# Attention outputs taken in alternating halves, and a distance penalty moved from a matrix product to VectorE

## The chip, the cores and the metric

The kernel runs on one core of one Trainium2 chip. The time is the device time of one execution in microseconds (us); of the kernel before three runs are known, with a median of 1116.42 us (1116.35 to 1116.87). The trace of one further, profiled execution gives what every engine did: PE is TensorE's matrix product, PEld its weight load, DVE is VectorE, ACT ScalarE, POOL GpSimd, SP the engine that issues most DMAs.

## The reference, cut to what matters

Two layers; each has a half-step SwiGLU feed-forward, a token mixer with two attention branches, and a second feed-forward. There are 256 tokens of width 1024, all in float32. Only the mixer is touched:

```python
def gqa_attention(q, k, v):            # branch A: 8 query heads, 2 key/value heads of 64
    sc = einsum(q, k) * 64 ** -0.5
    p = softmax(sc)
    return einsum(p, v)

def diff_attention(q, k, v, lam, slopes):   # branch B: 4 heads, two softmax maps each
    dist = abs(qpos[:, None] - kpos[None, :])
    bias = -slopes[:, None, None] * dist[None]
    sc = einsum(q, k) * 64 ** -0.5
    p = softmax(sc + bias[None, None])
    w = p[:, 0] - lam * p[:, 1]
    return einsum(w, v)
```

`slopes` is 2^(-2), 2^(-4), 2^(-6), 2^(-8) for the four heads.

## The kernel before

Weights arrive from HBM in tiles of 128x2048 float32. Each half tile (128x1024) is split in two: ScalarE rounds it to a short format (`whi`, line 307) and VectorE subtracts to get the remainder (`wlo`, line 308). A product is then three TensorE matmuls (lines 85 to 87). A planner written in plain Python (`pump`, `done`, `half`) keeps a fixed number of half tiles split ahead of TensorE. VectorE also forms the conditioning vectors from their own weight stream (line 240: a multiply and a sum in one instruction over 128x1024).

In a mixer the projections come first, then the attention pieces are emitted by hand between the sixteen halves of the gate product (`gate_mm`, rows named `gt`): scores of branch A (`a_scores`, rows `sc`), transposes of its probabilities (`a_T`, `pt` into `pT`), its outputs (`a_pv`, `ot`); scores of branch B (`b_scores`, `scb`), their normalisation on VectorE (`b_norm`, `xb`), transposes (`b_T`, `wt`), outputs (`b_out`, `od`). Each engine runs its own instructions in order; a scheduler decides the order on each engine when the kernel is built, and PSUM banks and SBUF buffers are handed out from pools. `gen` is a pool of four PSUM banks that `sc`, `pt`, `ot`, `scb` and `wt` share, so a later tile waits until an earlier one has been read.

`a_pv(jj)` (line 855) makes eight float32 matmuls whose results have 64 rows: for key/value head v=0 they go to PSUM rows 0 to 63, for v=1 to rows 64 to 127. The profiler records each float32 matmul as two instructions, so a call shows as sixteen. All of v=0 is emitted before all of v=1. It runs twice in each layer.

`b_scores(pair, t)` (lines 879 to 898) works on two heads, called four times in each layer. For each head one matmul of a scaled identity (`idn`) with the distances (`dist`) puts the penalty for both maps in a PSUM bank, 128x512; twelve matmuls of 64 contraction rows add the scores of both heads. VectorE then takes the maximum of the bank (line 892), scales it by 0.125 (line 894), and ScalarE takes the exponential from PSUM into `xb` (line 898).

Of the kernel before, what the change touches and what calls it, by code (L numbers as in the profile page):

```python
# [14 lines left out]
F32R = mybir.dt.float32r  # L15
AF = mybir.ActivationFunctionType
ALU = mybir.AluOpType
AX = mybir.AxisListType

P = 128  # L20
D = 1024
S = 256
# [19 lines left out]
def trunk(tc, a):  # L42
    nc = tc.nc
    with (
# [11 lines left out]
        def nm(s):  # L56
            uid[0] += 1
            return f"{s}_{uid[0]}"

        def gen(name="gen"):  # L60
            return ps.tile([P, 512], F32, tag="gen", bufs=4, name=nm(name))
# [4 lines left out]
        def b2(name, shape=(P, 512), dt=F32):  # L66
            return sb.tile(list(shape), dt, tag="b2", bufs=NB2, name=nm(name))

        def slot(name, shape, dt=F32, kind="a"):

            live[kind] += 1
            assert live["w"] + live["a"] <= NSLOT, (name, live)
            return wp.tile(list(shape), dt, tag="w4", bufs=NSLOT, name=nm(name))
# [4 lines left out]
        def small(name, shape, bufs=6):  # L78
            return sb.tile(list(shape), F32, tag=f"sm{int(np.prod(shape[1:]))}", bufs=bufs, name=nm(name))

        def const(name, shape, dt=F32):
            return sb.tile(list(shape), dt, tag=name, bufs=1, name=name)
# [25 lines left out]
        ident = const("ident", [P, P])  # L108
# [5 lines left out]
        for hf in range(2):  # L114
            x = slice(hf * 512, (hf + 1) * 512)
# [12 lines left out]
        def cols(l, s):  # L128
            return [("col", l, s, w, u) for u in range(4) for w in (1, 0)]
# [33 lines left out]
        for l, s in SUBS:  # L163
            w = weights(l, s)
            ad = list(ada_in[(l, s)])
            if (l, s) == (0, 0):
                c = cols(0, 0)
# [347 lines left out]
        def later(ins):  # L515
            follow(ins, after[0])
# [23 lines left out]
        def ffn(i, nT, norm1, first, nT_next):  # L540
# [56 lines left out]
            for idx in range(start, NS):  # L597
                g, u = gen("g"), gen("u")
                gate_up_mm(g, u, unit(idx), nT)
                hT[idx] = gate_up_act(g, u)  # L600
                if idx == 1:
                    hT[0] = first_T(hts)
                elif idx - 1 < NS - TAIL:
                    if idx == 2 and first is None:
                        down(0)
                    down(idx - 1)
                if idx == 4 and s == 0:
                    consts = mixer_loads(l)
                if idx == 7:
                    gate_bcast(l, s)  # L610
                    if s == 0:
                        consts = mixer_consts(l, consts)
# [15 lines left out]
        mc = {}  # L628

        def mixer_loads(l):  # L630
            if not mc:
                for name in ("cos", "sin"):
                    mc[name] = const(name, [P, 2, 64])
                    later(nc.scalar.dma_start(mc[name], a[name]))
                d = b2("dist", (P, 2, S))
                later(nc.scalar.dma_start(d, a["dist"]))
                mc["dist"] = const("dist", [P, 2, S], F32R)
                nc.scalar.copy(mc["dist"], d)
            g = sb.tile([P, 2, 64], F32, tag="qkg", bufs=1, name=nm("qkg"))
            later(nc.scalar.dma_start(g.rearrange("p a b -> p (a b)"), a["qk_g"][l:l + 1, :].broadcast_to([P, P])))  # L640
            lp = sb.tile([P, 256], F32, tag="lp", bufs=1, name=nm("lp"))
            later(nc.scalar.dma_start(lp, a["lam_p"][l:l + 1, :].broadcast_to([P, 256])))
            bg = sb.tile([P, 16], F32, tag="bg", bufs=1, name=nm("bg"))
            later(nc.scalar.dma_start(bg, a["b_gate_col"][l]))
            sg = sb.tile([P, 1], F32, tag="subg", bufs=1, name=nm("subg"))
            later(nc.scalar.dma_start(sg, a["subln_col"][l]))
            return g, lp, bg, sg
# [38 lines left out]
        def mixer(i, nT, norm1, consts, nT_next):  # L686
            l = SUBS[i][0]
            nh, nl = nT
            dist = mc["dist"]
            C, Sn, bg, subg, lam = consts  # L690
            cap_w[0] = CAP0

# [156 lines left out]

            def a_pv(jj):  # L850
                ot = gen("ot")
                for v in range(2):
                    for i in range(2):
                        for c in range(2):
                            nc.tensor.matmul(ot[v * 64:(v + 1) * 64, i * 256:(i + 1) * 256], va[:, c, v * 64:(v + 1) * 64],
                                             pTs[i, v][:, c * 256:(c + 1) * 256], start=(c == 0), stop=(c == 1))
                if jj == 0:
                    st["oa"] = (slot("oaH", (P, 4, S), F32R), slot("oaL", (P, 4, S), F32R))
                oH, oL = (x[:, 2 * jj:2 * jj + 2, :] for x in st["oa"])
                ov = ot.rearrange("p (i x) -> p i x", i=2)  # L860
                nc.scalar.copy(oH, ov)
                nc.vector.tensor_tensor(oL, ov, oH.bitcast(F32), op=ALU.subtract)


            idns = mc.setdefault("idn", [])
            for hd in range(len(idns), 4):
                idns.append(const(f"idn{hd}", [P, P], F32R))
                nc.scalar.mul(idns[hd], ident, -8.0 * 2.0 ** (-8.0 * (hd + 1) / 4.0))
            xs = {}
            wTs = {}  # L870

            def b_scores(pair, t):

                tok = slice(t * P, (t + 1) * P)
                scs = []
                for hd in (2 * pair, 2 * pair + 1):
                    sc = gen("scb")

                    nc.tensor.matmul(sc.rearrange("p (m k) -> p m k", m=2), idns[hd], dist[:, t:t + 1, :].broadcast_to([P, 2, S]),
                                     start=True, stop=False, skip_group_check=True)  # L880
                    scs.append(sc)
                for m in range(2):
                    ch = m * 2 + pair
                    for x, y in ((0, 0), (1, 0), (0, 1)):
                        for e in range(2):
                            pr = slice(e * 64, (e + 1) * 64)
                            nc.tensor.matmul(scs[e][:, m * 256:(m + 1) * 256], st["qdT"][x][pr, ch, tok], st["kdT"][y][pr, ch, :],
                                             start=False, stop=y == 1, skip_group_check=True)
                for e, sc in enumerate(scs):
                    x = b2("xb")  # L890
                    nm_ = small("nmx", (P, 2))
                    nc.vector.tensor_reduce(nm_, sc.rearrange("p (m k) -> p m k", m=2), axis=AX.X, op=ALU.max, negate=True)
                    bi = small("bi", (P, 2))
                    nc.vector.tensor_scalar(bi, nm_, 0.125, None, op0=ALU.mult)
                    sm = small("sum", (P, 2))
                    for m in range(2):
                        y = slice(m * 256, (m + 1) * 256)
                        nc.scalar.activation(x[:, y], sc[:, y], AF.Exp, bias=bi[:, m:m + 1], scale=0.125, accum_out=sm[:, m:m + 1])
                    xs[2 * pair + e, t] = (x, sm)

            def b_norm(pair, t):
# [120 lines left out]
            vd1 = proj("vd", 1)  # L1022
            a_norm(1, 0)
            a_pv(0)
            nc.scalar.copy(st["vd"][:, 1, :], vd1)
            a_scores(1, 1)
# [3 lines left out]
            gate_mm(0, 1)  # L1030
            a_norm(1, 1)
            b_scores(0, 0)
            gate_mm(1, 0)
            a_T(1, 0)
            gate_mm(1, 1)
            a_T(1, 1)
            b_norm(0, 0)
            b_scores(0, 1)
            gate_mm(2, 0)
            a_pv(1)  # L1040
            gate_mm(2, 1)
            b_norm(0, 1)
            b_scores(1, 0)
            gate_mm(3, 0)
            b_T(0)
# [181 lines left out]
        for i, (l, s) in enumerate(SUBS):  # L1227
            nxt = new_nT() if i + 1 < len(SUBS) else None
            if s == 1:
                norm1 = mixer(i, nT, norm1, consts, nxt)  # L1230
            else:
                norm1, consts = ffn(i, nT, norm1, (lambda *x, nT=nT: first(nT, *x)) if i == 0 else None, nxt)
            nT = nxt
# [78 lines left out]
```

## Time and profile before

| what | value |
|---|---|
| median of three runs | 1116.42 us |
| the profiled execution, its own time | 1117.3 us |
| its span, first to last instruction | 1115.5 us |
| PE busy in the span | 1097.5 us |
| DVE busy | 865.4 us |
| ACT busy | 587.7 us |
| mixer of the first layer, attention part | about 242 to 316 us |
| mixer of the second layer, attention part | about 783 to 861 us |

Times in the trace are counted from the first instruction. A row of the timeline gives start, duration, engine, line, operation, the output and inputs by the names in the program, and how many instructions were merged in it; matmuls overlap, so durations of single matmuls add up to more than the time that they take, and the distance between starts is what counts.

### The profile page before, as it was taken

What the parts mean: (1) busy time and instruction counts of PE and PEld (TensorE: products, weight loads), DVE (VectorE), ACT (ScalarE), POOL (GpSimd) and SP (SyncE); (2) the same over time, 40 slices, a digit from 0 to 9 for tenths busy, and PEclk for the clock granted to TensorE, in tenths of its full rate; (3) what the DMA queues carried; (4) which work ended last, traced back from release to release, by engine and by line L of the source; (5) the groups of instructions that cost most, each with busy time, mean ns of one, the idle gap of its engine ahead of it and who ended that gap; (6) DMA issues with size and microseconds to landing.
All of it is one profiled execution on the core that took longest, in us unless ns stands there. A gap on an engine that the chain in (4) does not pass through costs nothing.

```text
span 1115.5 us, 19105 instructions
## 1 busy us (share of the span) xinstructions
PE 1097.5 (98%) x7774; PEld 1013.2 (91%) x7774; DVE 865.4 (78%) x1330; ACT 587.7 (53%) x911; POOL 44.3 (4%) x52
## 2 busy tenths in 40 slices
PE   6999999999999999999999999999999999999997
PEld 5989999898899899999989999989889998999996
DVE  6997986899968798886589886569987879765543
ACT  5463484568664644536365545435776547444432
POOL 1000000220010000000000000004000000000000
PEclk9999999999999999999999999999999999999999
DMA  9999986378745298897449977543765454876501
GB/s 337 385 355 323 346 328 221 125 266 321 263 153 189 79 374 348 332 353 290 149 155 363 350 296 266 197 157 137 282 226 187 152 190 180 309 265 224 195 18 38
DMA packets 42584, 271.11 MB, mean 243 GB/s; under 512 B 5624, under 2 KB 6392, under 8 KB 12544
## 3 DMA queue, kind: packets, MB, share of 16 engines
q1 hardware_dynamic: 40036, 267.93, 64.8%
q10 hardware_dynamic: 2460, 1.96, 0.6%
q8 instruction: 61, 1.00, 0.3%
q14 instruction: 27, 0.22, 0.1%
HBM read 268.82 MB, written 1.05 MB: 242 GB/s over the span
## 4 chain that ended last, share of the span: by engine, by line
PE 88%; DVE 7%; DMA 2%; ACT 1%; issue 1%; POOL 0%; SPq 0%; POOLq 0%; DVEq 0%; ACTq 0%
PE dn L87 7%; PE dn L86 7%; PE dn L85 7%; PE u L85 6%; PE g L85 6%; PE u L87 6%; PE g L87 6%; PE g L86 6%; PE u L86 6%; PE gt L85 2%; PE gt L87 2%; PE gt L86 2%; DVE wlo L308 2%; PE g L1184 2%; PE u L1184 2%; PE yb L87 1%
## 5 line engine op out<-in xcount | busy, mean ns | idle before, releaser
L308 DVE TENSOR_TENSOR wlo<-raw,whi 128x1024 fp32r<-128x1024 f32 x364 | 437.2, 1221 | 139.7 <-PE u L86 86.7
L307 ACT CAST whi<-raw 128x1024 fp32r<-128x1024 f32 x364 | 373.7, 1052 | 214.1 <-PE u L87 83.4
L85 PE MATMUL g<-nh,whi 128*128 128x256 f32 x592 | 166.2, 281 | 0.0
L85 PE MATMUL u<-nh,whi 128*128 128x256 f32 x592 | 166.1, 281 | 0.0
L87 PE MATMUL u<-nl,whi 128*128 128x256 f32 x592 | 165.9, 280 | 0.0
L86 PE MATMUL g<-nh,wlo 128*128 128x256 f32 x592 | 165.9, 280 | 0.0
L87 PE MATMUL g<-nl,whi 128*128 128x256 f32 x592 | 165.9, 280 | 0.0
L86 PE MATMUL u<-nh,wlo 128*128 128x256 f32 x592 | 165.9, 280 | 0.0
L85 PE MATMUL dn<-whi,hh 128*128 128x512 f32 (+1 forms) x358 | 138.3, 386 | 0.0
L86 PE MATMUL dn<-whi,hl 128*128 128x512 f32 (+1 forms) x358 | 138.1, 386 | 0.0
L87 PE MATMUL dn<-wlo,hh 128*128 128x512 f32 (+1 forms) x358 | 138.1, 386 | 0.0
L240 DVE CUSTOM_DVE_ANT_0 raw<-raw,cb 128x1024 f32<-128x1024 f32 x96 | 114.7, 1219 | 1.5 <-DMA raw<-in_ada_t_dram 1.5
L87 PEld LDWEIGHTS u<-nl,whi 128*128 128x128 f32 x592 | 113.0, 191 | 0.1
L87 PEld LDWEIGHTS g<-nl,whi 128*128 128x128 f32 x592 | 113.1, 191 | 0.0
L86 PEld LDWEIGHTS g<-nh,wlo 128*128 128x128 f32 x592 | 111.3, 188 | 1.3
L85 PEld LDWEIGHTS g<-nh,whi 128*128 128x128 f32 x592 | 111.1, 188 | 1.4
L86 PEld LDWEIGHTS u<-nh,wlo 128*128 128x128 f32 x592 | 111.3, 188 | 0.0
L85 PEld LDWEIGHTS u<-nh,whi 128*128 128x128 f32 x592 | 111.1, 188 | 0.1
L521 ACT ACTIVATE sg<-g 128x512 f32<-128x512 f32 x41 | 24.5, 597 | 106.4 <-PE g L87 103.9
L87 PEld LDWEIGHTS dn<-wlo,hh 128*128 128x128 f32 x358 | 67.2, 188 | 13.6
L85 PEld LDWEIGHTS dn<-whi,hh 128*128 128x128 f32 x358 | 67.3, 188 | 12.3
L86 PEld LDWEIGHTS dn<-whi,hl 128*128 128x128 f32 x358 | 67.3, 188 | 12.3
(211 smaller groups left out, 2026.0 us busy)
## 6 DMA issues: line engine op xcount, KB each, us to landing
raw<-in_w_gu_dram SPq DMA_DIRECT2D x79, 1024.0 KB, 5.1
raw<-in_w_d_dram SPq DMA_DIRECT2D x41, 1024.0 KB, 6.1
raw<-in_ada_t_dram SPq DMA_DIRECT2D x40, 1024.0 KB, 6.1
raw<-in_ada_g_dram SPq DMA_DIRECT2D x24, 1024.0 KB, 5.7
raw<-in_w_in_dram SPq DMA_DIRECT2D x16, 1024.0 KB, 4.9
raw<-in_w_gate_dram SPq DMA_DIRECT2D x16, 1024.0 KB, 4.9
raw<-in_w_gu_dram SPq DMA_DIRECT2D x18, 512.0 KB, 6.8
raw<-in_ada_t_dram SPq DMA_DIRECT2D x16, 512.0 KB, 7.5
```

The costliest lines, as they stand in the source:

```text
L85: nc.tensor.matmul(out, Lh, Rh, start=start, stop=False, skip_group_check=True)
L86: nc.tensor.matmul(out, Ll, Rh, start=False, stop=False, skip_group_check=True)
L87: nc.tensor.matmul(out, Lh, Rl, start=False, stop=stop, skip_group_check=True)
L240: queue("dve", nc.vector.tensor_tensor_reduce(r, r, cb, 1.0, 0.0, op0=ALU.mult, op1=ALU.add, accum_out=col[:, k:k + 1]))
L307: queue("act", nc.scalar.copy(hi, r))
L308: queue("dve", nc.vector.tensor_tensor(lo, r, hi.bitcast(F32), op=ALU.subtract))
L521: nc.scalar.activation(sg, g, AF.Silu)
L1184: nc.tensor.matmul(bank[:, c * 256:(c + 1) * 256], W[:, w], N[:, k, :], start=x + y + k + c == 0, stop=y == 1 and k == NK - 1, skip_group_ ...
```

## The change

In `a_pv` the loop over v becomes the innermost, so that matmuls for rows 0 to 63 and for rows 64 to 127 alternate. In `b_scores` the two penalty matmuls of a call go; the first of the score matmuls starts the bank. In place of one maximum over 128x512, VectorE runs two instructions over 128x256 for each head: each adds a constant penalty from SBUF (`pen`) to the scores from PSUM, writes the sum to `xb` in SBUF and leaves the maximum. ScalarE then takes the exponential from `xb` in place. The four scaled identities (four ScalarE instructions of 128x128 at the start) and the rounded `dist` (one of 128x512) go; four ScalarE instructions of 128x512 make `pen` when the mixer's constants are loaded in the first feed-forward.

```diff
-                mc["dist"] = const("dist", [P, 2, S], F32R)
-                nc.scalar.copy(mc["dist"], d)
+                mc["pen"] = const("pen", [P, 4, 2, S])
+                for hd in range(4):
+                    nc.scalar.mul(mc["pen"][:, hd], d, -8.0 * 2.0 ** (-8.0 * (hd + 1) / 4.0))
...
                 ot = gen("ot")
-                for v in range(2):
-                    for i in range(2):
-                        for c in range(2):
+                for i in range(2):
+                    for c in range(2):
+                        for v in range(2):
                             nc.tensor.matmul(ot[v * 64:(v + 1) * 64, i * 256:(i + 1) * 256], va[:, c, v * 64:(v + 1) * 64],
                                              pTs[i, v][:, c * 256:(c + 1) * 256], start=(c == 0), stop=(c == 1))
...
-            idns = mc.setdefault("idn", [])
-            for hd in range(len(idns), 4):
-                idns.append(const(f"idn{hd}", [P, P], F32R))
-                nc.scalar.mul(idns[hd], ident, -8.0 * 2.0 ** (-8.0 * (hd + 1) / 4.0))
...
-                scs = []
-                for hd in (2 * pair, 2 * pair + 1):
-                    sc = gen("scb")
-                    nc.tensor.matmul(sc.rearrange("p (m k) -> p m k", m=2), idns[hd], dist[:, t:t + 1, :].broadcast_to([P, 2, S]),
-                                     start=True, stop=False, skip_group_check=True)
-                    scs.append(sc)
+                scs = [gen("scb") for _ in range(2)]
...
-                                             start=False, stop=y == 1, skip_group_check=True)
+                                             start=x + y == 0, stop=y == 1, skip_group_check=True)
                 for e, sc in enumerate(scs):
                     x = b2("xb")
-                    nm_ = small("nmx", (P, 2))
-                    nc.vector.tensor_reduce(nm_, sc.rearrange("p (m k) -> p m k", m=2), axis=AX.X, op=ALU.max, negate=True)
+                    mx = small("mx", (P, 2))
+                    for m in range(2):
+                        y = slice(m * 256, (m + 1) * 256)
+                        nc.vector.tensor_tensor_reduce(x[:, y], sc[:, y], pen[:, 2 * pair + e, t, :], 1.0, -3.0e38,
+                                                       op0=ALU.add, op1=ALU.max, accum_out=mx[:, m:m + 1])
                     bi = small("bi", (P, 2))
-                    nc.vector.tensor_scalar(bi, nm_, 0.125, None, op0=ALU.mult)
+                    nc.vector.tensor_scalar(bi, mx, -0.125, None, op0=ALU.mult)
                     sm = small("sum", (P, 2))
                     for m in range(2):
                         y = slice(m * 256, (m + 1) * 256)
-                        nc.scalar.activation(x[:, y], sc[:, y], AF.Exp, bias=bi[:, m:m + 1], scale=0.125, accum_out=sm[:, m:m + 1])
+                        nc.scalar.activation(x[:, y], x[:, y], AF.Exp, bias=bi[:, m:m + 1], scale=0.125, accum_out=sm[:, m:m + 1])
```

The order of the instructions, from the program, at three places in the first layer's mixer. Numbers behind a name tell one tile from another and differ between the two programs.

TensorE at the first call of `a_pv`; `pT` are the transposed probabilities (before 2869 and 2913 for v=0, 2876 and 2920 for v=1), `va` the values. Before:

```order
L855 MATMUL ot_3008<-pT_2869,va_2252 64x256 x2
L855 MATMUL ot_3008<-pT_2913,va_2252 64x256 x2
L855 MATMUL ot_3008<-pT_2876,va_2252 64x256 x2
L855 MATMUL ot_3008<-pT_2920,va_2252 64x256 x2
L809 MATMUL sc_3022<-kaT_2250,qaT_2476 128x256
```

And now (2864 and 2908 for v=0, 2871 and 2915 for v=1):

```order
L858 MATMUL ot_3003<-pT_2864,va_2255 64x256
L858 MATMUL ot_3003<-pT_2871,va_2255 64x256
L858 MATMUL ot_3003<-pT_2864,va_2255 64x256
L858 MATMUL ot_3003<-pT_2871,va_2255 64x256
L858 MATMUL ot_3003<-pT_2908,va_2255 64x256
L858 MATMUL ot_3003<-pT_2915,va_2255 64x256
L858 MATMUL ot_3003<-pT_2908,va_2255 64x256
L858 MATMUL ot_3003<-pT_2915,va_2255 64x256
L811 MATMUL sc_3017<-kaT_2253,qaT_2471 128x256
```

The same eight matmuls now change the half of PSUM's rows each time; what stands before and behind is the same.

TensorE at the second call of `b_scores` in the layer, behind the last transposes of branch A's probabilities. Before:

```order
L844 MATMUL pt_3248<-ident,p_3048 128x128 x2
L879 MATMUL scb_3267<-dist,idn_2253 128x512
L887 MATMUL scb_3267<-kd_2850,qd_2643 128x256
L887 MATMUL scb_3267<-kd_2850,qd_2644 128x256
L879 MATMUL scb_3269<-dist,idn_2255 128x512
L887 MATMUL scb_3269<-kd_2850,qd_2643 128x256
L887 MATMUL scb_3269<-kd_2850,qd_2644 128x256
L887 MATMUL scb_3267<-kd_2851,qd_2643 128x256
```

And now:

```order
L846 MATMUL pt_3243<-ident,p_3043 128x128 x2
L880 MATMUL scb_3262<-kd_2845,qd_2638 128x256
L880 MATMUL scb_3263<-kd_2845,qd_2638 128x256
L880 MATMUL scb_3262<-kd_2845,qd_2639 128x256
L880 MATMUL scb_3263<-kd_2845,qd_2639 128x256
L880 MATMUL scb_3262<-kd_2846,qd_2638 128x256
```

The penalty matmuls are gone, and the two heads' scores alternate from the first; at the other seven calls they alternated already, behind the two penalty matmuls.

ScalarE shortly before that, between the exponentials of the first call's two heads (before `xb_3145` and `xb_3153`, now `xb_3138` and `xb_3147`) and the copies of transposed probabilities to SBUF. Before:

```order
L898 ACTIVATE xb_3145,sum_3150<-scb_3129,bi_3148 128x256 x2
L898 ACTIVATE xb_3153,sum_3158<-scb_3131,bi_3156 128x256 x2
L847 COPY pT_3199<-pt_3194 128x512
L847 COPY pT_3206<-pt_3201 128x512
L978 ACTIVATE gt_3118<-gt_3161,bg_1116 128x256 x2
```

And now:

```order
L894 ACTIVATE xb_3138,sum_3144<-xb_3138,bi_3142 128x256 x2
L849 COPY pT_3194<-pt_3189 128x512
L849 COPY pT_3201<-pt_3196 128x512
L894 ACTIVATE xb_3147,sum_3153<-xb_3147,bi_3151 128x256 x2
L974 ACTIVATE gt_3113<-gt_3156,bg_1119 128x256 x2
```

Both copies have moved ahead of the second head's exponentials.

## Rows read from the trace of the kernel before

**Rows 1.** The page, part 1: busy time, share, instructions of each engine.
```profile
PE 1097.5 (98%) x7774; PEld 1013.2 (91%) x7774; DVE 865.4 (78%) x1330; ACT 587.7 (53%) x911; POOL 44.3 (4%) x52
```
**Rows 2.** Waits of PE: who, for whom, us in total, times, longest us.
```profile
PE pt L844 <- ACT xb L898: 0.3, 1, 0.3
```
**Rows 3.** Timeline of PE at the first `a_pv`, the second row from a narrower window.
```profile
264.34 2.86 PE L855 MATMUL ot<-pT,va 128*64 128x256 f32 x16
...
264.82 0.81 PE L855 MATMUL ot<-pT,va 128*64 128x256 f32 x3
```
**Rows 4.** The same call by windows, `ot` alone: PE busy (records), PEld, DVE, ACT.
```profile
264.34:265.26 0.92, 0.92 (x5) 0.60 (x6) 0.00 (x0) 0.00 (x0) 1.00 0.87 365
265.26:266.12 0.86, 0.86 (x9) 0.72 (x8) 0.00 (x0) 0.00 (x0) 1.00 0.38 86
```
**Rows 5.** Timeline of PE at the first `b_scores`, behind a gate product.
```profile
273.46 0.28 PE L87 MATMUL gt<-nl,whi 128*128 128x256 f32 x1
273.58 0.62 PE L879 MATMUL scb<-dist,idn 128*128 128x512 f32 x2
...
275.04 0.38 PE L85 MATMUL gt<-nh,whi 128*128 128x256 f32 x1
```
**Rows 6.** Timeline of PE around branch A's scores, between two projection products.
```profile
242.19 0.28 PE L87 MATMUL pt<-nl,whi 128*128 128x256 f32 x1
...
243.27 0.38 PE L85 MATMUL pt<-nh,whi 128*128 128x256 f32 x1
```
**Rows 7.** Timeline of PE at the fourth `b_scores`, behind transposes.
```profile
301.28 0.60 PE L915 MATMUL wt<-ident,xb 128*128 128x128 f32 x4
...
303.18 0.38 PE L85 MATMUL gt<-nh,whi 128*128 128x256 f32 x1
```
**Rows 8.** Timeline of PE around scores of branch A behind transposes, second layer.
```profile
802.19 1.03 PE L844 MATMUL pt<-ident,p 128*128 128x128 f32 x8
...
804.05 0.51 PE L481 MATMUL pj<-whi,nh 128*128 128x512 f32 x1
```
**Rows 9.** Timeline of PE at the second `b_scores`, first layer.
```profile
281.60 0.60 PE L844 MATMUL pt<-ident,p 128*128 128x128 f32 x4
282.46 0.66 PE L844 MATMUL pt<-ident,p 128*128 128x128 f32 x4 [0.26 <-ACT xb L898]
...
285.13 0.39 PE L85 MATMUL gt<-nh,whi 128*128 128x256 f32 x1
```
**Rows 10.** Timeline of DVE: a maximum over 128x512 of PSUM, and what follows.
```profile
279.45 0.68 DVE L892 TENSOR_REDUCE nmx<-scb 128x2 f32<-128x512 f32 x1
280.05 1.21 DVE L240 CUSTOM_DVE_ANT_0 raw<-raw,cb 128x1024 f32<-128x1024 f32 x1
```
**Rows 11.** Timeline of DVE: two-input instructions with a running result, two lengths.
```profile
6.92 0.69 DVE L354 CUSTOM_DVE_ANT_0 sq<-h 128x512 f32<-128x512 f32 x1 [6.92 <-DMA h<-in_x_dram]
...
7.54 0.69 DVE L354 CUSTOM_DVE_ANT_0 sq<-h 128x512 f32<-128x512 f32 x1
...
8.28 1.22 DVE L240 CUSTOM_DVE_ANT_0 raw<-raw,cb 128x1024 f32<-128x1024 f32 x1
```
**Rows 12.** Timeline of ACT where the distances are prepared.
```profile
97.11 0.62 ACT L638 CAST dist<-dist 128x512 fp32r<-128x512 f32 x1 [0.98 <-DMA dist<-in_dist_dram]
...
107.97 0.60 ACT L521 ACTIVATE sg<-g 128x512 f32<-128x512 f32 x1 [7.47 <-PE g L87]
```
**Rows 13.** Windows of both attention parts: us, then PE, PEld, DVE, ACT busy.
```profile
267.86:308.55 40.69, 40.43 (x341) 36.57 (x338) 38.96 (x94) 27.36 (x67) 0.00 (x0) 1.00 0.76 277
813.30:852.68 39.38, 39.38 (x336) 36.08 (x334) 35.23 (x83) 27.09 (x67) 0.00 (x0) 1.00 0.58 206
```
**Rows 14.** Timeline of DVE: the start of that stretch, and `xb` of its last call.
```profile
267.86 0.69 DVE L862 TENSOR_TENSOR oaL<-ot,oaH 128x512 fp32r<-128x512 f32 x1 [0.99 <-ACT oaH L861]
...
308.07 0.48 DVE L909 SCALAR_TENSOR_TENSOR xb<-xb,rs 128x256 f32<-128x256 f32 x1
```
**Rows 15.** Timeline of PE: the transposes that take this `xb`.
```profile
311.47 0.60 PE L915 MATMUL wt<-ident,xb 128*128 128x128 f32 x4
```

More of the change, by code (lines that the diff above doesn't have):

```diff
@@ L688, in mixer @@
             nh, nl = nT
-            dist = mc["dist"]
+            pen = mc["pen"]
             C, Sn, bg, subg, lam = consts
```

## The prediction

> **What bounds the kernel now.** I read the page's busy times first. PE is busy for 1097.5 of 1115.5 us, DVE for 865.4, ACT for 587.7 [rows 1]: TensorE has hardly a gap anywhere, so an instruction taken from it is worth its whole distance to the next one, as long as the others keep up. The second view is the list of PE's waits: in both attention parts it names one wait for branch B, 0.3 us for an exponential [rows 2]. The third is the timeline of PE at each place that the change touches, and the last, windows over the attention parts, which show how much room VectorE has. In the first layer's stretch, from the first `ot` to the last `xb`, VectorE works 38.96 of 40.69 us; in the second layer's 35.23 of 39.38 [rows 13]. The question is whether VectorE can follow a TensorE that comes earlier while it gets more work itself.
>
> **The outputs of branch A.** One call takes sixteen records, 2.86 us to the end of the last [rows 3]. Single records take 0.38, so from the first start to the last it is 2.48. Three consecutive records of one half take 0.81, so within a half one starts (0.81 - 0.38) / 2 = 0.216 after the other [rows 3]. Sixteen in a row would need over 15 x 0.216 = 3.24; the trace has less because the halves already overlap in part. In the first 0.92 us there are 5 records, in the next 0.86 there are 9 [rows 4]: at 0.216 one half gives 4 in that time, so both halves run side by side there at full rate, and the second half begins 0.92 behind the first. Eight records of one half span 2.48 - 0.92 = 1.56. With alternating halves both start together, the call's last start comes at 1.56, and 0.92 us go in each call. There are four calls (the records are 64 in all, 16 in each): **3.7 us**. The bounds: no gain if something else than the order held the second half back; a loss if changing halves at each matmul cost them their overlap, since then the spacing gives 0.27 + 14 x 0.216 = 3.3 against 2.48, 0.8 more in each call. I take the full gain, since the overlap that is there shows 9 records at the same spacing.
>
> [...]
>
> **The penalty product.** At the first call of `b_scores` the last gate matmul starts at 273.46 and the next gate matmul at 275.04: 1.58 us for the penalty and the scores [rows 5]. The same twelve score matmuls without a penalty stand between two products in branch A: 242.19 to 243.27, 1.08 us [rows 6]. So a call behind a gate product gives 0.50; there are four. Behind transposes: four transposes start at 301.28, the last at 301.28 + 0.60 - 0.27 = 301.61, and the gate product goes on at 303.18, 1.57 later [rows 7]; in branch A it is 804.05 - (802.19 + 1.03 - 0.27) = 1.10 [rows 8], where 0.27 is the duration of one transpose. That gives 0.47, and there are three such calls. The eighth is the first layer's second call. From the start of its eight transposes to the gate product it takes 285.13 - 281.60 = 3.53 [rows 9]; the like in branch A takes 804.05 - 802.19 = 1.86 [rows 8]. The difference of 1.67 holds a wait of 0.26 for a PSUM bank [rows 2, 9] and slow changes between penalty and scores. The bank is now read by VectorE's sum instead of the exponential, and ScalarE copies the transposes ahead of the second exponential, so both causes go. Sum: 4 x 0.50 + 3 x 0.47 + 1.67 = **5.1 us**.
>
> **What VectorE gets.** Out: one maximum for each head, 280.05 - 279.45 = 0.60 start to start [rows 10]. In: two sums with maximum over 128x256, one input in PSUM. The trace has no such instruction. The nearest multiply and sum in one go: over 512 columns 7.54 - 6.92 = 0.62 start to start, the read of its result included; durations 0.69 for 512 and 1.22 for 1024 [rows 11], so 512 columns cost 0.53 and the rest of the 0.62 is 0.09 fixed. For 256 that makes 0.27 + 0.09 = 0.36. Bounds for one: 0.30, half of the maximum (no more work than before), and 0.62, as long as the one of twice its length. I take 0.35, since the two lengths lie on one line: 0.70 for a head against 0.60, 0.10 more, 0.8 us more in each layer for its eight heads.
>
> [...]
>
> Does this reach TensorE? The last call of the first layer decides. Its first head's `xb` ends at 308.55 and the transposes need it at 311.7 (the third of four from 311.47) [rows 14, 15]: a margin of 3.1. TensorE comes there earlier by 2 x 0.92 + 0.50 + 1.67 + 0.50 + 0.47 = 5.0. VectorE's stretch starts earlier by 0.92, since at 267.86 it had waited 0.99 for the `ot` of that call [rows 14], it has 1.73 of idle time to give [rows 13], and 0.8 of new work: 1.85 earlier at best. 3.1 - 5.0 + 1.85 is about zero. Some of the idle time will stay, so I put a stall of 0.3 us there. In the second layer TensorE comes 3.8 earlier (two outputs, two calls of each kind), and VectorE has 4.15 idle [rows 13]: no stall. The weight remainders that VectorE makes in between are used long after; they wait for nothing new.
>
> **Small pieces.** The penalty tables cost ScalarE four instructions where one of 0.62 stood; three more add 1.9 us at 97 us. ScalarE waits 7.47 us soon after, for TensorE [rows 12], which hides them. Without that cover it would be 1.9. The exponential reads SBUF instead of PSUM: I cost that at nothing, ScalarE being busy 27 of 40 us there [rows 13].
>
> **The sum.** 3.7 + 5.1 - 0.3 = 8.5 less. The profiled execution took 1117.3 with a span of 1115.5: 1.8 lie around the span and stay. That gives 1108.8 for it. It was 0.9 above the median of 1116.42; from the median the sum is **1107.9 us**.
>
> **Rivals.**
> 1. VectorE's new instruction is as slow as its upper bound, 0.62, so a head costs 0.64 more than before and a layer 5.1, which is 4.3 above my 0.8. In the first layer all of it becomes a stall of TensorE at the last transposes; in the second most is taken by idle time, I put 1. Time: 1107.9 + 4.3 + 1 = 1113.2. For it: VectorE is full in the first layer. Against: the two lengths on one line.
> [...]
> 3. Alternating halves lose their overlap: 4 x 0.8 lost in place of 3.7 gained, 1107.9 + 6.9 = 1114.8. For it: no row shows an order that changes halves at each matmul in this shape. Against: where the two halves meet now, both keep their 0.216 [rows 3, 4].
> 4. Slower: the sum with maximum takes over 0.75 for 256 columns. Then a head costs 0.9 more than the maximum did, a layer 7; the first layer stalls by about 6, the second, after 4 of idle time, by 3, and the 8.8 are eaten. At 0.85 each it would be 0.2 x 8 x 2 = 3.2 above before, 1119.6. For it: no row shows a running maximum with a PSUM input in this form. Against: the plain maximum reads PSUM at 0.60 for 512.
> 5. The change is not what it says, or the saved time is given back where weights are short: 1116.4. Against: TensorE hardly waits anywhere.
>
> **How the numbers follow.** Forecast 70% (1107.2 to 1109.0: stall between nothing and 1); program order 12%; slow sum 9%; lost overlap 4%; slower 2%; nothing 3%. The range of 8 in 10 takes in the forecast and the second rival and a part of the first: 1107.2 to 1110.2. A difference of 0.2%, 2.2 us, is what a measurement can tell from none. Faster by more: 0.95; within it: 0.03; slower: 0.02.
>
> **What would show it.** In the new trace each `ot` call spans about 1.9 us instead of 2.86, with two records at nearly the same start; no penalty rows; the gate product goes on 1.1 us behind the last product in front of each `scb`; the sums with maximum follow each other by 0.35. A wait of PE for `xb` at the fourth transposes of the first layer longer than 1 us would show that VectorE is late. I am wrong if the sums take 0.5 or more, or if `ot` keeps its 2.86.

## The result, and the profile after

| | before | changed |
|---|---|---|
| time, median (range) of 4 runs each | 1116.38 us (1115.39 to 1116.87) | 1108.39 us (1107.98 to 1109.12) |
| ratio to before | 1 | 0.9925, 95% interval 0.9911 to 0.9939 |
| profiled execution: time, span | 1117.3, 1115.5 us | 1109.12, 1107.3 us |

The changed kernel is 8.0 us faster; 8.5 were forecast, and 1107.9 us. Busy times, the page's part 1 after (before: [rows 1]):

```profile
PE 1089.7 (98%) x7758; PEld 1008.1 (91%) x7758; DVE 865.4 (78%) x1378; ACT 588.7 (53%) x910; POOL 44.2 (4%) x52
```

TensorE loses 7.8 us of work and stays at 98%. VectorE has 48 instructions more and the same busy time. Now TensorE at the three kinds of place, first layer, in the timeline after (start, duration, engine, line, operation, count): the first `a_pv`, the second call of `b_scores`, and the last transposes with the outputs behind them.

```profile
264.01 1.95 PE L858 MATMUL ot<-pT,va 128*64 128x256 f32 x16
...
279.89 1.04 PE L846 MATMUL pt<-ident,p 128*128 128x128 f32 x8
280.86 0.98 PE L880 MATMUL scb<-kd,qd 64*128 64x256 f32 x12
281.77 0.39 PE L85 MATMUL gt<-nh,whi 128*128 128x256 f32 x1
...
309.99 0.60 PE L911 MATMUL wt<-ident,xb 128*128 128x128 f32 x4
310.43 1.50 PE L924 MATMUL od<-vd,wT 128*128 128x128 f32 x12
312.11 0.71 PE L924 MATMUL od<-vd,wT 128*128 128x128 f32 x4 [0.17 <-ACT wT L915]
```

The sixteen `ot` records take 1.95 where they took 2.86 [rows 3]. From the eight transposes to the gate product it is 281.77 - 279.89 = 1.88 where it was 3.53 [rows 9]: the penalty, the slow changes and the wait for a bank [rows 2] are gone. New in the last two lines is that the outputs wait, for a copy of `wT`. Windows over `ot` alone (us, PE busy and records) show how the two halves now run from the first moment:

```profile
264.01:264.93 0.92, 0.92 (x10) 0.63 (x12) 0.00 (x0) 0.00 (x0) 1.00 0.83 321
```

Ten records start in the first 0.92 us; it was five [rows 4]. VectorE in the same kernel, its timeline at the first layer's last call:

```profile
301.68 0.41 DVE L887 CUSTOM_DVE_ANT_0 xb<-scb,pen 128x256 f32<-128x256 f32 x1
...
302.02 0.41 DVE L887 CUSTOM_DVE_ANT_0 xb<-scb,pen 128x256 f32<-128x256 f32 x1
302.37 0.08 DVE L887 DVE_READ_ACCUMULATOR2_ANT mx<- 128x1 f32 x1
302.37 1.22 DVE L308 TENSOR_TENSOR wlo<-raw,whi 128x1024 fp32r<-128x1024 f32 x1
303.51 0.15 DVE L890 TENSOR_SCALAR bi<-mx 128x2 f32<-128x2 f32 x1
```

The sums follow each other by 0.34 and 0.35 us; 0.35 was forecast. The last two lines show what else stands in this queue: a weight remainder of 1.22 us got between the maximum and the bias made of it, so the exponential of this head starts 1.1 us later than it could. ScalarE's row there waits for that bias:

```profile
303.76 0.51 ACT L894 ACTIVATE xb<-xb,bi 128x256 f32<-128x256 f32 x1 [1.75 <-DVE bi L890]
```

The windows over both attention parts after (us, PE, PEld, DVE, ACT busy) answer to [rows 13]:

```profile
264.80:303.90 39.10, 39.10 (x353) 36.13 (x350) 37.82 (x112) 27.23 (x63) 0.00 (x0) 1.00 0.78 278
811.26:847.00 35.74, 35.74 (x320) 33.66 (x319) 33.02 (x105) 26.29 (x67) 0.00 (x0) 1.00 0.62 219
```

VectorE is idle for 1.28 us in the first layer and for 2.72 in the second.

### The profile page after: what moved, and what is told of

It is laid out like the page before. It is cut to its first block, busy times and chain, and to the rows that moved or that the text cites. A ratio compares the mean times of both kernels' runs of the same rounds, so it can differ in the third digit from the quotient of the medians.

```text
span 1107.3 us, 19106 instructions
## 1 busy us (share of the span) xinstructions
PE 1089.7 (98%) x7758; PEld 1008.1 (91%) x7758; DVE 865.4 (78%) x1378; ACT 588.7 (53%) x910; POOL 44.2 (4%) x52
## 4 chain that ended last, share of the span: by engine, by line
PE 90%; DVE 5%; ACT 2%; DMA 1%; issue 1%; POOL 0%; POOLq 0%; SPq 0%
PE dn L87 7%; PE dn L86 7%; PE dn L85 7%; PE g L85 6%; PE u L85 6%; PE g L87 6%; PE u L87 6%; PE g L86 6%; PE u L86 6%; PE g L1180 2%; PE u L1180 2%; PE gt L85 2%; PE gt L87 2%; PE gt L86 2%; PE yb L87 1%; PE yb L86 1%
```

## The experiments

Whole times scatter by about a microsecond, and so do profiles: in code that no kernel here changes, the first 64 us, TensorE comes to the same matmul between 0.96 us earlier and 1.33 later than in before's profile. So parts of a microsecond are read stage by stage: the start of one and the same matmul in both traces, and how that difference grows from 263 to 345 us (first layer) and from 805 to 850 us (second) of before's profile. In the first layer it splits into the removed work (single distances between matmuls that shrank by over 0.08 us, all at changed calls), stalls (distances that grew by over 0.03) and the rest (many matmuls a few nanoseconds further apart). Microseconds, minus is earlier; the kernels are told of below.

```
kernel                         removed  stalls   rest |  first layer | second layer
changed, profile of the result  -4.81    0.67    0.26 |    -3.88     |    -3.76
changed, once more              -4.81    0.00    0.24 |    -4.57     |    -3.76
alternating halves alone        -1.83    0.00    0.48 |    -1.35     |    -1.91
penalty alone                   -2.98    0.00    0.24 |    -2.74     |    -1.94
halves in pairs                 -4.71    0.62    0.22 |    -3.87     |    -3.67
minimum gives the bias          -4.81    0.28    0.22 |    -4.31     |    -3.76
cut products                    -4.47    0.00    0.32 |    -4.15     |    -3.76
remainders on GpSimd            -4.35    6.19    0.31 |     2.15     |    -3.76
minimum and GpSimd              -4.36    5.33    0.26 |     1.23     |    -3.76
sums twice                        (not split)         |     3.76     |    -1.52
```

**Each part alone.** The first kernel takes from the change only the order of the loops in `a_pv`:

```
-                for v in range(2):
-                    for i in range(2):
-                        for c in range(2):
+                for i in range(2):
+                    for c in range(2):
+                        for v in range(2):
```

> The kernel before with the alternating order in a_pv alone; the penalty product stays. Theory (TensorE sets the time, and the order alone held the second half back): each of the four calls loses the 0.91 us that the changed kernel's trace shows, 3.6 in all, about 1112.7 us; ot spans 1.95 to the end of its last record. Rival (what comes earlier is lost at the next wait, the one for a PSUM bank in front of the second b_scores): the first layer's first call gives nothing, 2.7 in all, about 1113.6.

1114.46 us against 1117.26 (ratio 0.997, interval 0.9959 to 0.998). Before stood 0.8 higher on this chip, and by that the time is the rival's. The trace is not: each call gives its 0.91 to 0.92, but this profile's start-up was 1.3 us later than before's, and the first layer gives 0.48 back in the rest. What the median of seven runs lacks beyond that, one profile does not show. A whole time does not separate 3.6 us from 2.7; the distance between neighbours does. The second kernel takes only the penalty's move, all other lines of the diff:

> The changed kernel with the old order in a_pv: the penalty on VectorE alone. Theory (a product that goes is worth its distance on TensorE): 7 x 0.46 + 1.65 = 4.9 less, about 1111.5; no wait for xb at the transposes of the first layer, since TensorE reaches them 1.8 later than in the changed kernel. Rival (VectorE's new work is paid in the first layer in any case): the wait of 0.3 and the later copy behind it stay, 4.2 less, about 1112.2.

1112.25 us (0.9954, 0.9941 to 0.9966): 5.0 less, with no stall, as the theory had it. Its calls give 2.98 in the first layer and its net in the second is 1.94. The removed work of both parts, 1.83 and 2.98, adds up to the 4.81 of the whole change: they don't hinder each other on TensorE.

**What the order of the halves does.** The loops again, each half's two products together, the halves changing only then:

```
                 for i in range(2):
-                    for c in range(2):
-                        for v in range(2):
+                    for v in range(2):
+                        for c in range(2):
```

> The changed kernel with the loops of a_pv in the order i, v, c: two matmuls (four records) of one half, then two of the other. Theory (a record of the free half may start while up to three records wait ahead of it): the fifth record starts with the first, a call spans nearly what alternation gives (last start at 1.6 to 1.8 us), time within 0.8 of the changed kernel's, 1108.4 to 1109.2. Rival (records start in program order): 0.70 behind for each change of half, last start at 2.7 us, more than before the change: 4 x 1.13 more than the changed kernel, about 1112.9.

1109.89 us (0.993, 0.9917 to 0.9944); less the 0.8 that before stood higher on this chip, it is in the theory's range. The call in its timeline, and its first 0.02 us by a window over `ot` alone (us, PE busy and records):

```profile
265.51 2.00 PE L858 MATMUL ot<-pT,va 128*64 128x256 f32 x16
...
265.51:265.53 0.02, 0.02 (x2) 0.02 (x2) 0.00 (x0) 0.00 (x0) 1.00 0.00 0
```

2.00 us against 1.95. The second half has four records of the first ahead of it here. If matmuls started strictly in order, the rival of this run, its first would come 3 x 0.216 = 0.65 us behind (spacing of [rows 3]); in the trace it comes 13 to 14 ns behind in all four calls (two records run in the first 0.02 us), so that rival falls: these matmuls of the two halves do not start in the order of the program, and what stands ahead of the prediction, that each engine runs its own instructions in order, does not hold for them. In pairs three records of the first half have still to start when the second half does; in the old order the second half started as the fifth record of eight did [rows 4], again with three to come. What held the second half back until then is not shown.

**How much room VectorE has.** Each sum is issued twice:

```
-                        nc.vector.tensor_tensor_reduce(x[:, y], sc[:, y], ...
+                        for _ in range(2):
+                            nc.vector.tensor_tensor_reduce(x[:, y], sc[:, y], ...
```

> The changed kernel with each sum with maximum issued twice (the second writes the same values again): 0.70 us more on VectorE for each head, 5.6 in each layer. Theory (VectorE has nothing left in the first layer, and in the second about its idle 2.5 us): stalls of 4.5 to 5.6 and of 2 to 3, about 1115.5 us, waits of PE at the transposes wt. Rival (VectorE has room, and 0.1 or 0.8 a head are the same to TensorE): under 1 us more, below 1109.4.

1119.62 us (1.0024, 1.0012 to 1.0036), some 11 above the changed kernel for 32 x 0.35 = 11.2 us of work on VectorE. Expected was 7, with most of it at the transposes `wt`. At the pair where the prediction looked for a stall (0.51 us from the start of the gate product ahead of it, where 0.11 is usual) it loses 0.4; the large losses of the first layer come later, at the gate's broadcast (`gb`). TensorE, then VectorE in this kernel's timeline:

```profile
328.59 0.28 PE L87 MATMUL gt<-nl,whi 128*128 128x256 f32 x1
330.31 0.49 PE L281 MATMUL gb<-gh,onesr 128*128 128x512 f32 x1 [1.44 <-ACT gh L279]
332.16 0.50 PE L282 MATMUL gb<-gl,onesr 128*128 128x512 f32 x1 [1.35 <-DVE gl L280]
```

```profile
327.88 1.23 DVE L308 TENSOR_TENSOR wlo<-raw,whi 128x1024 fp32r<-128x1024 f32 x1
...
329.68 1.22 DVE L308 TENSOR_TENSOR wlo<-raw,whi 128x1024 fp32r<-128x1024 f32 x1
...
331.42 0.69 DVE L280 TENSOR_TENSOR gl<-gacc,gh 128x512 fp32r<-128x512 f32 x1
```

`gl` stands behind remainders that had been pushed back. Behind these waits the granted clock is lower, 0.67 from 333 to 338 us, with 1.00 from 326 to 328.8 and from 338 to 342; a window of the same kernel (us, PE busy, PEld, DVE, ACT, POOL, granted clock):

```profile
333.00:338.00 5.00, 5.00 (x31) 4.90 (x30) 0.59 (x1) 1.36 (x3) 0.95 (x1) 0.67 0.06 25
```

Of the 7.6 us that this kernel loses against the changed one in the first layer, 2.8 lie ahead of the broadcast, 3.1 at it and 1.7 behind it, in the stretch with the clock of 0.67. The 2.8 are not waits alone: the scheduler also gave TensorE another order here, with scores and transposes taken apart by gate products, so this kernel is no clean measure of VectorE's room. What it does show is that here a late VectorE is paid mainly where the next thing that TensorE needs stands behind the heap (4.8 of the 7.6 us at the broadcast and behind it), not where the work was added.

**Less work between maximum and exponential.** The sum is scaled by -0.125 and runs a minimum, so what it accumulates is the bias, and 16 small instructions go:

```
+                        nc.vector.tensor_tensor_reduce(x[:, y], sc[:, y], pen[:, 2 * pair + e, t, :], -0.125, 3.0e38,
+                                                       op0=ALU.add, op1=ALU.min, accum_out=bi[:, m:m + 1])
...
-                    nc.vector.tensor_scalar(bi, mx, -0.125, None, op0=ALU.mult)
...
+                        nc.scalar.activation(x[:, y], x[:, y], AF.Exp, bias=bi[:, m:m + 1], scale=-1.0, ...
```

> The changed kernel with its sum taken times -0.125 and a running minimum in place of the maximum, so that the accumulated value is the bias itself and the 16 small products that made it go from VectorE (and the wait between maximum and exponential gets shorter). Theory (VectorE is full in the first layer and what it is late there is paid at the last transposes, at the outputs that wait for ScalarE's copies, and later at the gate): TensorE gets back most of what the first layer gives back, 0.3 to 0.8 us, and nothing in the second layer: 0.5 us below the changed kernel. Rival (what the first layer gives back is a matter of the matmuls' spacing alone): no difference, and the gap ahead of the outputs stays at 0.45 us.

> The changed kernel once more, on the chip of the run with the minimum, so that the two stand beside each other: both theories expect 0.9925 of the kernel before, within 0.2%.

The recorded ratio to before is 0.9924 for both (intervals 0.9911 to 0.9938 and 0.9911 to 0.9936; medians 1109.77 and 1108.62 against 1117.72 us): no difference that can be measured, so this theory of the 0.5 us has no support. The changed kernel's second profile told more. It has no stall at all: the outputs follow the transposes at once.

```profile
309.72 0.60 PE L911 MATMUL wt<-ident,xb 128*128 128x128 f32 x4
310.16 1.95 PE L924 MATMUL od<-vd,wT 128*128 128x128 f32 x16
311.86 0.37 PE L85 MATMUL gt<-nh,whi 128*128 128x256 f32 x1
```

The two profiles of this one kernel part on VectorE 37 us before. The profile of the result, then the second:

```profile
273.40 0.16 DVE L831 RECIPROCAL rs<-sum 128x2 f32<-128x2 f32 x1
274.74 1.23 DVE L240 CUSTOM_DVE_ANT_0 raw<-raw,cb 128x1024 f32<-128x1024 f32 x1 [1.18 <-DMA raw<-in_ada_t_dram]
```

```profile
273.38 0.16 DVE L831 RECIPROCAL rs<-sum 128x2 f32<-128x2 f32 x1
273.46 1.20 DVE L240 CUSTOM_DVE_ANT_0 raw<-raw,cb 128x1024 f32<-128x1024 f32 x1
```

Where the weights of the adaptive norm land late, VectorE stands for 1.18 us in front of a product that nobody is waiting for, and from 266.6 to 303.9 us it gets 36.09 us of work done where the second profile has 37.29. In four full profiles VectorE's wait for such weights in this stretch and TensorE's stalls go together: 1.2 and 0.67 us, none and none, 1.1 and 0.62 (halves in pairs), 1.7 and 0.28 (the minimum, with less work on VectorE). No run changes the landing alone, so this is read from the profiles and not tested.

**Room for VectorE, in two ways.** Seven of the products over 1024 columns cut to 8 columns:

```
+COL0, COL1 = 41, 48
...
+            w = 8 if COL0 <= ncol[0] - 1 < COL1 else 1024
+            queue("dve", nc.vector.tensor_tensor_reduce(r[:, 0:w], r[:, 0:w], cb[:, 0:w], 1.0, 0.0, ...
```

> The changed kernel with seven of VectorE's 1.22 us products over 1024 columns (weight columns of the adaptive norm, at 280 to 298 us of the first layer) cut to 8 columns each, so part of that layer's scale and shift is not computed; TensorE's work is the same. VectorE gets 8 us of room there. Theory (what the first layer gives back of the 4.98 us of its parts is VectorE's lateness): from 263 to 345 us of before's profile TensorE then gains 4.9 to 5.0 us, no gap of 0.45 ahead of the outputs, against 3.9 and 4.6 in two profiles of the changed kernel; about 0.5 us off the time. Rival (the matmuls' own spacing gives it back, whatever VectorE does): 3.9 to 4.6 as before. The second layer stays at 3.76.

1109.58 us (0.9931, 0.9915 to 0.9948): not faster, and the first layer's 4.15 us is no more than the rival's. Two things are told apart by it. The stalls are gone, although VectorE now waits 3.9 us for weights in this stretch: with room, the late weights cost nothing at the last transposes (stalls 0.00). But 4.9 was wrong, since the "rest" stays (0.32), and one scores call lost 0.34. TensorE, then ScalarE in this kernel:

```profile
282.09 1.32 PE L885 MATMUL scb<-kd,qd 64*128 64x256 f32 x12
```

```profile
281.33 0.49 ACT L899 ACTIVATE xb<-xb,bi 128x256 f32<-128x256 f32 x1
...
281.82 0.56 ACT L854 COPY pT<-pt 128x512 f32<-128x512 f32 x1
```

The call takes 1.32 where it took 0.98. Its second head's first product starts at 282.43, just behind the end of the copy at 282.38, and the semaphore it waits for is ScalarE's, which fits a bank of `gen` that this copy had still to read. Here the scheduler put the second head's exponentials ahead of that copy; in the changed kernel both copies come first. So part of what the second call gave rests on an order that the scheduler need not choose. The other way: four weight remainders are made by GpSimd:

```
+LOS = (95, 96, 97, 98)
...
-                    queue("dve", nc.vector.tensor_tensor(lo, r, hi.bitcast(F32), op=ALU.subtract))
+                    if nlo[0] - 1 in LOS:
+                        nc.gpsimd.tensor_tensor(lo, r, hi.bitcast(F32), op=ALU.subtract)
+                    else:
+                        queue("dve", nc.vector.tensor_tensor(lo, r, hi.bitcast(F32), op=ALU.subtract))
```

> The changed kernel with four weight remainders of the first layer's attention (287 to 302 us) made by GpSimd, which has nothing to do there, in place of VectorE: 4.9 us of room without leaving work out. Theory: as for the cut products, TensorE gains 4.9 to 5.0 us from 263 to 345 us and the time goes 0.4 to 0.7 us below the changed kernel. Rival: GpSimd's instruction holds VectorE up while it runs, or its remainders come too late for the matmuls that use them; then nothing is gained or TensorE waits for wlo.

> Both reliefs together, the minimum that gives the bias at once and the four remainders on GpSimd. Theory: no more than the remainders alone, 4.9 to 5.0 us from 263 to 345 us, since TensorE cannot gain more than its own removed work. Rival: less, where GpSimd holds VectorE up.

1114.56 us (0.998, 0.9971 to 0.9989) and, with the minimum, 1114.69 (0.9976, 0.9967 to 0.9985): 6 us lost, and the rival is right. GpSimd's and VectorE's timelines in the former:

```profile
284.38 3.30 POOL L313 TENSOR_TENSOR wlo<-raw,whi 128x1024 fp32r<-128x1024 f32 x1 [51.31 <-DVE mx L894]
292.55 2.55 POOL L313 TENSOR_TENSOR wlo<-raw,whi 128x1024 fp32r<-128x1024 f32 x1 [4.88 <-ACT whi L310]
299.95 5.36 POOL L313 TENSOR_TENSOR wlo<-raw,whi 128x1024 fp32r<-128x1024 f32 x2 [4.85 <-ACT whi L310]
```

```profile
285.37 2.34 DVE L897 TENSOR_SCALAR bi<-mx 128x2 f32<-128x2 f32 x1
...
300.44 2.62 DVE L912 SCALAR_TENSOR_TENSOR xb<-xb,rs 128x256 f32<-128x256 f32 x1
302.98 2.35 DVE L910 TENSOR_TENSOR c<-rs,nlam 128x1 f32<-128x1 f32 x1
...
305.76 0.49 DVE L912 SCALAR_TENSOR_TENSOR xb<-xb,rs 128x256 f32<-128x256 f32 x1
```

What VectorE began while a GpSimd subtraction ran, but for the reads of a running result (0.08 to 0.09 us), ended at its end or up to 0.3 us behind it: the same instruction on `xb` takes 2.62 and 0.49 us, and the product over one column 2.35, where it takes 0.14 to 0.16 at other places of this timeline. It reaches TensorE twice. The fourth scores call gives its 0.46 back, since its second head's first product waits for VectorE's sum of the call before, which stands behind an `xb` of 2.49 us and ends only at 296.95 (the product starts at 297.01); and the transposes then wait 3.43 us for `xb`:

```profile
306.51 0.38 PE L918 MATMUL wt<-ident,xb 128*128 128x128 f32 x2
310.32 0.69 PE L918 MATMUL wt<-ident,xb 128*128 128x128 f32 x2 [3.43 <-DVE xb L912]
```

No kernel here beats the changed one.

## Why the prediction was right, step by step

- **The outputs of branch A, 3.7 us.** Right: 0.91 to 0.92 a call, four calls, 3.65 (the second layer's two give 1.84 in the kernel that has this part alone). The overlap that the prediction read from nine records in 0.86 us [rows 4] was there from the start. The prediction's second rival, program order at 12%, which the range takes in, rests on a term that no run shows: a call gives 0.91 to 0.92 where the halves alternate, and even in pairs the second half starts 13 to 14 ns behind the first.
- **The penalty, 5.1.** 4.8: 2.98 in the first layer, of which 1.61 at the second call (1.67 forecast), and about 1.85 at the second layer's four calls. A call gives 0.46, whatever stands ahead of it, where 0.50 and 0.47 were forecast. The yardstick, branch A's scores, was a little short: 1.08 and 1.10 [rows 6, 8], where a call without its product takes 1.11 to 1.12 from matmul to matmul. So this term was 0.27 too large in all.
- **VectorE's sum, 0.35 each.** Right, and with it the rivals of a slower sum, 0.62 and over 0.75, fell. The kernel with the sums twice suggests that they would have cost more than the prediction put, since in it lateness goes on to the gate's broadcast (3.1 us) and to the clock of 0.67 behind it (1.7). An instruction of before that comes near the sum is the `SCALAR_TENSOR_TENSOR` on `xb` with two float32 inputs: over 256 columns it starts at 308.07 [rows 14] and the next instruction, below, 0.40 later, which is closer to the 0.36 of one line through both lengths than to the 0.62 of the upper bound.

```profile
308.47 0.16 DVE L905 RECIPROCAL rs<-sum 128x2 f32<-128x2 f32 x1
```

- **A stall of 0.3 us at the last transposes of the first layer, none in the second.** The margin of about zero was there. Of the profile of the result, VectorE's `xb` and the transposes of the last call:

```profile
306.43 0.48 DVE L905 SCALAR_TENSOR_TENSOR xb<-xb,rs 128x256 f32<-128x256 f32 x1
...
306.71 0.70 PE L911 MATMUL wt<-ident,xb 128*128 128x128 f32 x4
```

This `xb` ends at 306.91, 1.64 earlier than before (1.85 at best was forecast), and the third transpose starts at 306.97. But the stall there is 0.11, and the size of 0.3 holds only as a mean, which is partly luck: 0.67 in this profile and nothing in the next, which goes with when a block of weights landed. Of the 0.67, 0.44 come at the outputs behind the transposes that follow, through ScalarE's copy of `wT`, which the prediction did not name, and 0.12 at the transposes of the call before.

- **Missed: the rest, about 0.25 us in the first layer.** It is in every kernel that is split in the table, with either part alone too. It comes mainly behind the last scores call, where 72 matmuls of the gate take 8.59 us up to the transposes and took 8.29 (below). Before has a single profile, so chance in that one is not excluded.
- **The small pieces at nothing.** Right: between 64 and 120 us, over the penalty tables, the difference to before changes by 0.03 us. The exponential takes 0.49 to 0.52 us from SBUF where it took 0.46 to 0.48 from PSUM, with room on ScalarE.
- **The sum, 8.5.** The two profiles of the changed kernel have spans 8.2 and 8.5 us shorter than before's 1115.5; the medians give 8.0 and, on the other chip, 9.1. The two changed stretches give 7.64 and 8.33 of the spans' difference; the remaining 0.6 and 0.2 lie outside them. By the terms as measured (3.65 + 4.83 - 0.3 - 0.25) the sum would be 7.9. The forecast's 0.5 us beyond the first median is within what the start-up alone scatters.

## What to carry to other kernels

Here products whose results go to different halves of PSUM's rows ran side by side from the first record on where they alternate (1.95 us a call) or stand in groups of four records (2.00), and only from 0.92 us on where eight records of one half stand ahead (2.86): interleave them, or keep to short groups. Where TensorE has no gaps, time its instructions by the distance from neighbour to neighbour with and without them; that gave each call here to 0.06 us. On a full engine (VectorE here, 37.82 of 39.10 us) look for work that nobody is waiting for (here a product for whose weights VectorE waited 1.18 us) ahead of work that is waited for, and do not move it to GpSimd without looking at what VectorE's instructions beside it then take (here 2.62 us for one of 0.49).

## What the runs showed of the hardware

**What VectorE began beside a GpSimd subtraction ended with it or up to 0.3 us behind it**, as above, 2.62 us for an instruction of 0.49; a 128x1024 subtraction takes GpSimd 2.55 us in the second of its rows, 3.30 in the first, which began beside a VectorE product of 1024 columns, and takes VectorE 1.22.

**One stream of matmuls ran at two speeds, 0.113 and 0.118 us a matmul, at the same granted clock.** The gate's 256-column matmuls behind the last scores call of the first layer, before and after:

```profile
309.31 0.28 PE L87 MATMUL gt<-nl,whi 128*128 128x256 f32 x1
...
310.33 0.28 PE L87 MATMUL gt<-nl,whi 128*128 128x256 f32 x1
```

```profile
303.76 0.28 PE L87 MATMUL gt<-nl,whi 128*128 128x256 f32 x1
...
305.18 0.28 PE L87 MATMUL gt<-nl,whi 128*128 128x256 f32 x1
```

1.02 us for nine, 0.113 each; 1.42 for twelve, 0.118 each, with a granted clock of 1.00 in both. The 72 matmuls from that call to the transposes take 8.29 us before and 8.59 after, 0.30 more, where the rest of this profile is 0.26 in all; every other kernel whose first layer is split above has a rest of 0.22 to 0.48, the one with the alternating halves alone included. Elsewhere, too, two executions of the same code differ: from 45 to 60 us before runs 130 matmuls and the changed kernel 135, with TensorE busy throughout at a granted clock of 1.00. What decides it stays open.

**A wait of 3.43 us is paid, and then a granted clock of 0.50 to 0.52.** Windows of the kernel with GpSimd's remainders (us, PE busy, PEld, DVE, ACT, POOL, granted clock):

```profile
306.00:309.40 3.40, 0.90 (x8) 0.66 (x6) 3.33 (x17) 1.43 (x5) 0.00 (x0) 0.94 0.39 154
309.40:312.00 2.60, 1.68 (x8) 1.68 (x9) 2.08 (x7) 2.60 (x8) 0.00 (x0) 0.50 0.79 243
312.00:316.00 4.00, 4.00 (x22) 4.00 (x21) 2.29 (x2) 2.18 (x3) 0.00 (x0) 0.52 0.39 129
```

After the wait the granted clock is 0.50 and then 0.52, while TensorE works without a gap from 312 to 316 us: 22 records in 4 us, where the next 4 us, at 1.00 again, have 38. Of the 6.19 us of stalls 3.59 are the wait itself; of the other 2.60 these 4 us alone make about 1.7, an estimate from the two counts, (38 - 22) x 4 / 38. In the kernel with the sums twice two waits of 1.44 and 1.35 us had the like behind them (0.67 over 5 us, above).
